# A two-layer decoder trunk on one core: where copies, low parts, value writes and filler steps stand inside the attention's passes over the heads

## The chip, the core and the metric

The kernel runs on one core of one Trainium2 chip. A core has five engines that work side by side, each on its own list of instructions in the order in which they were written down: TensorE (PE in the profile, with the weight loads as PEld), VectorE (DVE), ScalarE (ACT), GpSimd (POOL) and SyncE (SP, which here only issues DMA transfers). Between engines only semaphores order the work: an instruction whose operand isn't ready holds up everything behind it on its own engine, and nothing on the others. The metric is the device time of one execution in microseconds.

## The reference

A trunk of two layers over 1024 tokens of width 1024. Layer 0 mixes with a short gated convolution, layer 1 with dilated attention; each is followed by a SwiGLU network of width 2816, and a norm ends it. All is float32. The part that matters here is the attention of layer 1, with 16 heads of width 64:

```python
BRANCHES = ((128, 1), (512, 4), (2048, 16))     # window, dilation

def dilated_branch(q, k, v, rel_bias, window, dilation):
    ...
    s = jnp.einsum("brnqhd,brnkhd->brnhqk", qb, kk) * (HEAD_DIM ** -0.5)
    ...
    s = s + bias                                # T5 bucket of the distance
    s = jnp.where(mask, s, NEG_INF)
    lse = jax.nn.logsumexp(s, axis=-1)
    p = jnp.exp(s - lse[..., None])
    o = jnp.einsum("brnhqk,brnkhd->brnqhd", p, vv)
    ...
    return o, lse

def dilated_attention_mixer(h, w_qkv, w_out, rel_bias):
    q, k, v = ...                               # h @ w_qkv, 16 heads of 64
    for window, dilation in BRANCHES:
        o, l = dilated_branch(q, k, v, rel_bias, window, dilation)
        ...
    alpha = jax.nn.softmax(jnp.stack(lses), axis=0)
    o = jnp.sum(alpha[..., None] * jnp.stack(outs), axis=0)
    return o.reshape(bsz, seq, D_MODEL) @ w_out
```

The weights alpha of the three branches and the three softmaxes fall together: the result of a head is the sum of exp(s) v over the entries of all branches, divided by the sum of exp(s) over all of them. The kernel computes it so, with one maximum, one unnormalised sum `o` and one denominator `z` for each head.

## The kernel before

**Precision.** A product of the projections and of the SwiGLU networks is taken in three matmuls, high x high, high x low and low x high, of operands split in two. `split` (line 132) makes the two: ACT copies the source into `hi` (line 142), DVE subtracts it from the source into `lo` (line 143). `take` (line 171) hands the next weight of a fixed list `ops` to a product, and has the one after it loaded, and split, ahead (`ensure`, line 163).

**The attention, head by head.** `slot(n, ...)` (line 1727) is called for n = 0 to 16. Slot n writes down the scores of head n, the softmax of head n, and the values products of head n-1, mixed with steps of other matmuls that fill TensorE while the softmax is under way.

- `scores` (line 1547): seven banks of matmuls (line 1560 and others), each read by DVE, which adds the bias into `lf`, `lh`, `ld`, `lp`; then the maximum over all of them (`m`, line 1611) and GpSimd's maximum over the partitions (`mb`, line 1614).
- `softmax`: DVE subtracts `mb` (line 1622), ACT takes exp in place (line 1623), five times.
- `values` (line 1626): products of exp(s) with the values `vx`, whose columns hold 64 values and 64 ones, into two banks, one for each half of the tokens. Lines 1633 are its matmuls. The first twelve go over `lf` and `lh`; then `j` runs over eight blocks of 128 keys with `ld` and `lp`, four for each bank. At the end ACT copies `z` and `o` of both halves out of the two banks (lines 1656 and 1657).
- `finish` (line 1660): `z` of a pair of heads goes through DRAM (`zdram`), is turned into its reciprocal and comes back broadcast; `attended` multiplies it on `o` and writes the result to `odram`.

**Values.** `value_tiles(g, j)` makes the values of head group g (four heads), half j of the tokens: four blocks of eight times three matmuls, each copied out by ACT (`v`, line 1508). After the fourth it writes `v` to DRAM (`vdram`) with four DMAs on GpSimd's queue (line 1512). `load_values` (line 1515) reads them back in another order into `vx`, six DMAs on SyncE's queue (line 1520); for the slots up to 14 it is called from `load_kq` (line 1525), at the head of every second slot, between the loads of the keys and of the queries of the next head.

**The filler.** `dense` (function `fill`) is one long generator that gives a few matmuls with each `next`, a filler step: projections of queries and keys, values, and at the end `out_product` (line 1819), the first half of the output projection, which for each of eight output tiles loads up to three tiles of `x` from `spill` on SyncE (line 1825), multiplies, and adds the bank to `x` (`add_to_x`, line 492). `slot` takes 15 filler steps; what is left when the last slot is done runs behind it (`run(dense)`, line 1868).

**The order inside a slot.** For n up to LAG = 13 a slot is lagged: a first loop of eight passes takes one step of the scores and one filler step each; a second loop takes two steps of the values products, and at pass 3 the whole softmax, with the filler steps that are left spread over its passes. Slots 14 and 15 put the values products into the first loop, and slot 14 (`late` = 3) has no filler step in the first passes.

**Slot 12** (n = LAG-1, the block 13 of the change's title). Before it, `load_attended` loads the first four attended tiles `oin` from `odram`; the generator `halves` splits them into `first`, one with each `next(hook)`, in the second loop from pass SOFT = 4 on, that is behind the softmax:

```python
                if i >= SOFT:
                    next(hook, None)
                other(left * (i + 1) // 8 - left * i // 8)
...
        for n in range(H):
            if n == LAG - 1:
                done.update(load_attended(range(AO)))
            hook = halves() if n == LAG - 1 else iter(())
            slot(n, dense, 15, 3 if n == H - 2 else 0, hook)
            run(hook)
```

The output product's steps read these splits. With 15 steps a slot, its first step falls into slot 12.

**Queues.** SyncE carries the loads of weights (`raw`), keys, queries, values, bias tables, attended tiles and `x`; GpSimd the writes of `vdram`, `zdram`, `odram` and the reads of the reciprocals, between its maxima. A DMA that waits holds up those behind it on its queue.

Of the kernel before, what the change touches and what calls it, by code (L numbers as in the profile page):

```python
# [20 lines left out]
H = 16  # L21
# [72 lines left out]
def view(t, off, dims):  # L94
    return bass.AP(tensor=t.tensor, offset=t.offset + off, ap=[t.ap[0]] + [list(d) for d in dims])
# [3 lines left out]
def trunk(ctx: ExitStack, tc: tile.TileContext, x, gains_in, cwi, ck, cwo, wqkv, wo, relb,  # L99
# [29 lines left out]
    scratch = consts.tile([128, 1], F32)  # L129
    zcol = consts.tile([128, 2, 1], F32)  # L130

    def split(src, dst=None, eng=nc.vector):

        w = src.shape[1]
        if dst is None:
            if w <= HALF:
                t = page("w", F32R)
                dst = t[:, :w], t[:, HALF:HALF + w]
            else:
                dst = page("w_hi", F32R)[:, :w], page("w_lo", F32R)[:, :w]  # L140
        hi, lo = dst
        nc.scalar.activation(hi, src, AF.Copy)  # L142
        eng.tensor_tensor(out=lo, in0=src, in1=hi, op=ALU.subtract)  # L143
        return hi, lo


# [16 lines left out]
    def ensure(upto):  # L163
        while op_state[0] < min(upto + 1, len(ops)):
            key = ops[op_state[0] + 1][0] if op_state[0] + 1 < len(ops) else None
            if key in sums_of:
                sums_of.pop(key)()
            made[op_state[0]] = ops[op_state[0]][1]()
            op_state[0] += 1

    def take(key, ahead=1):
        i = op_state[1]
        assert ops[i][0] == key, (ops[i][0], key)
        ensure(i + ahead)
        op_state[1] += 1
        return made.pop(i)
# [198 lines left out]
    def run(*gens):  # L375
        for _ in zip(*gens):
            pass
        for g in gens:
            for _ in g:
                pass  # L380
# [1082 lines left out]
    def blk(j):  # L1463
        return (j // 4) * HALF + (j % 4) * 8

    def attention(norm, qk):
# [23 lines left out]
        def value_tiles(g, j):  # L1490

            if j == 0:
                wv[:] = [take(("v", g, i), 0) for i in range(2)]
            v = page("v")
            for b4 in range(4):
                if j and b4 in (1, 2):
                    ensure(op_state[1] + b4 - 1)
                t = 4 * j + b4
                b = bank()[:, :256]
                for k in range(KT):  # L1500
                    (hi, lo), (whi, wlo) = qk.h[j][k], wv[k // 4]
                    a, c = slice(b4 * 128, b4 * 128 + 128), slice(k % 4 * 256, k % 4 * 256 + 256)
                    nc.tensor.matmul(b, hi[:, a], whi[:, c], start=k == 0, stop=False)  # L1503
                    nc.tensor.matmul(b, hi[:, a], wlo[:, c], start=False, stop=False)  # L1504
                    nc.tensor.matmul(b, lo[:, a], whi[:, c], start=False, stop=k == KT - 1)  # L1505
                    if k % 2:
                        yield
                nc.scalar.activation(v[:, b4 * 256:b4 * 256 + 256], b, AF.Identity, scale=norm.r[:, t:t + 1])
                yield
            vd = vdram[g]  # L1510
            for r in range(4):
                nc.gpsimd.dma_start(bass.AP(vd.tensor, vd.offset + (512 * j + r) * 256,
                                          [[16 * 256, 32], [4 * 256, 4], [1, 256]]), v[32 * r:32 * r + 32])

        def load_values(p):
            src = vdram[p // 2]
# [109 lines left out]
        def values(p, a, st):  # L1626
            lf, lh, ld, lp = (st[n] for n in ("lf", "lh", "ld", "lp"))
            acc = [bank(), bank()]
            kd = [[128, 4], [1, 32]]
            b1 = [[32, 16], [1, 8]]  # L1630

            def mm(ih, off, dims, u, rhs, first=False, last=False):
                nc.tensor.matmul(view(acc[ih], off, dims), vx[:, u, 64 * a:64 * a + 128], rhs,  # L1633
                                 start=first, stop=last)

            for ih in range(2):
                for r4 in range(4):
                    mm(ih, r4 * 32, kd, 8 + r4, view(lf, ih * HALF + r4 * 32, kd), first=r4 == 0)
                    if r4 % 2:
                        yield  # L1640
            for r4 in range(4):
                mm(1, r4 * 32, kd, 12 + r4, view(lh, r4 * 32, kd))
                if r4 % 2:
                    yield
            for j in range(8):
                off = (j % 4) * 8
                mm(j // 4, off, b1, j, view(ld, blk(j), b1), last=False)
                if j:
                    mm(j // 4, off, b1, j - 1, view(lp, blk(j), b1), last=j % 4 == 3)
                yield  # L1650
            o, z = st["o"], st["z"]
            n0 = slice(64 * a, 64 * a + 64)
            z0 = slice(64 - 64 * a, 128 - 64 * a)
            for ih in range(2):
                s = slice(ih * HALF, (ih + 1) * HALF)
                nc.scalar.activation(z[n0, s], acc[ih][z0], AF.Copy)
                nc.scalar.activation(o[n0, s], acc[ih][n0], AF.Copy)
            yield

        def finish(p):  # L1660
# [66 lines left out]
        def slot(n, dense, ndense, late=0, hook=iter(())):  # L1727

            def other(k):
                for _ in range(k):  # L1730
                    next(dense, None)

            p, a = divmod(n, 2)
# [55 lines left out]
            for i in range(8):  # L1789
                next(pv, None)  # L1790
                next(pv, None)
                if i == (2 if n > LAG + 1 else 5):
                    attended()
                if lagged and a and ending and i == 6:
                    next(ending[-1])
                if not lagged and (i < FIN0 or i > SOFT):
                    next(extra, None)
                if i in (1, 2):
                    next(later, None)
                if i == (3 if lagged else SOFT):  # L1800
                    if n < H:
                        live[n] = new
                        run(softmax(new))
                if i >= SOFT:
                    next(hook, None)
                other(left * (i + 1) // 8 - left * i // 8)
            run(pv)
# [36 lines left out]
        def fill():  # L1844
            for kind, g in FILL[1:]:
                if kind == "qk":
                    yield from projections(g)
                else:
                    for j in range(2):
                        yield from value_tiles(g, j)  # L1850
            yield from out_product(0, range(AO), first)
# [4 lines left out]
                yield  # L1856

        dense = fill()
        for n in range(H):
            if n == LAG - 1:  # L1860
                done.update(load_attended(range(AO)))
            hook = halves() if n == LAG - 1 else iter(())
            slot(n, dense, 15, 3 if n == H - 2 else 0, hook)
            run(hook)
        acts.update(split_attended(load_attended(range(AO, 7))))
        ensure(ahead_ao)
        slot(H, dense, 15)
# [201 lines left out]
```

## Time and profile before

| | us |
|---|---|
| three runs | 2140.9, 2142.98, 2143.33 |
| median | 2142.98 |
| the profiled execution, its own time | 2143.59 |
| its span, first to last instruction | 2141.5 |
| mean granted clock of TensorE in it | 0.994 |

The span is what the views of the trace cut up; the time of the execution is 2.1 us longer. Times in the views count from the span's start. In the rows of a timeline the idle time of the engine just before an instruction stands in brackets with what released it; a row in which consecutive instructions of one form are gathered gives their number behind an x and their total length. "SPq" and "POOLq" rows are the issues of DMAs on SyncE's and GpSimd's queues. A tile's name is that of the program (`bank<-lf,vx` is a matmul of `lf` and `vx` into a bank).

### The profile page before, as it was taken

To read this page: it belongs to the slowest core of one execution; us is meant where nothing else is said; L and a number is where in the kernel's file an instruction comes from. 1 tells how busy PE (TensorE), PEld (TensorE's weight loads), DVE (VectorE), ACT (ScalarE), POOL (GpSimd) and SP (SyncE) were. 2 spreads that over 40 slices of the span, in tenths; PEclk is the share of its full clock that TensorE was granted. 3 is DMA by queue.
4 is the path that set the end of the run, shared out by engine and by line. 5 is a ranking of instruction groups with operands and counts; after the bars stand their busy time and mean duration, and the time that the engine had idled before them with its cause. 6 is when DMAs were issued, how large, how long until landed. Compare 5 with 4: busy or idle time off the path is not lost.

```text
span 2141.5 us, 31004 instructions
## 1 busy us (share of the span) xinstructions
PE 2108.1 (98%) x11086; PEld 1807.9 (84%) x11086; DVE 1744.0 (81%) x3272; ACT 1007.4 (47%) x1848; POOL 254.2 (12%) x370
## 2 busy tenths in 40 slices
PE   9999999999999999999999999899999999999998
PEld 7788878888888888877899989888788888888887
DVE  8798769988888888868967687777998888888876
ACT  7333426444444564335545544545543434356435
POOL 1000000110101000000323333221010101001000
PEclk9999999999999999999999999999999999999999
DMA  7322642233332576340767678755223333368432
GB/s 218 93 94 69 226 133 75 103 102 106 113 109 99 173 218 194 112 161 33 263 206 182 180 193 226 212 179 163 69 93 102 107 109 106 106 201 240 156 94 79
DMA packets 143354, 304.90 MB, mean 142 GB/s; under 512 B 48943, under 2 KB 55327, under 8 KB 143201
## 3 DMA queue, kind: packets, MB, share of 16 engines
q1 hardware_dynamic: 107488, 201.94, 31.3%
q0 software_dynamic: 28080, 86.29, 12.7%
q10 hardware_dynamic: 7632, 14.70, 1.8%
q8 instruction: 88, 1.44, 0.3%
q14 instruction: 66, 0.53, 0.1%
HBM read 212.48 MB, written 83.05 MB: 138 GB/s over the span
## 4 chain that ended last, share of the span: by engine, by line
PE 82%; DVE 7%; issue 3%; ACT 2%; DMA 2%; POOL 1%; SPq 0%; DVEq 0%; POOLq 0%; ACTq 0%
PE bank L563 19%; PE bank L561 19%; PE bank L562 19%; PE bank L371 4%; PE bank L372 4%; PE bank L370 4%; PE bank L653 3%; PE bank L656 3%; PE bank L655 3%; PE bank L1633 2%; POOL mb L1614 1%; PE bank L1503 1%; PE bank L1504 1%; PE bank L1505 1%; DVE w L143 1%
## 5 line engine op out<-in xcount | busy, mean ns | idle before, releaser
L563 PE MATMUL bank<-b,w 128*128 128x512 f32 x1952 | 761.7, 390 | 5.5 <-DVE w L143 5.3
L561 PE MATMUL bank<-b,w 128*128 128x512 f32 x1952 | 763.3, 391 | 2.1 <-ACT w L142 1.7
L562 PE MATMUL bank<-b,w 128*128 128x512 f32 x1952 | 761.1, 390 | 0.6 <-DVE b L872 0.6
L563 PEld LDWEIGHTS bank<-b,w 128*128 128x128 f32 x1952 | 366.8, 188 | 86.4 <-DVE w L143 10.2
L561 PEld LDWEIGHTS bank<-b,w 128*128 128x128 f32 x1952 | 367.0, 188 | 78.7 <-ACT w L142 2.8
L562 PEld LDWEIGHTS bank<-b,w 128*128 128x128 f32 x1952 | 366.9, 188 | 77.0 <-DVE b L872 1.8
L142 ACT ACTIVATE w<-combo 128x512 fp32r<-128x512 f32 (+2 forms) x488 | 249.2, 540 | 232.0 <-DVE combo L190 215.1
L143 DVE TENSOR_TENSOR w<-combo,w 128x512 fp32r<-128x512 f32 (+2 forms) x488 | 276.2, 579 | 39.4 <-ACT w L142 38.7
L567 ACT ACTIVATE part<-bank 128x512 f32<-128x512 f32 x186 | 110.7, 596 | 390.2 <-PE bank L563 388.5
L143 DVE TENSOR_TENSOR w<-raw,w 128x512 fp32r<-128x512 f32 (+2 forms) x342 | 189.5, 575 | 38.7 <-ACT w L142 38.7
L571 DVE TENSOR_TENSOR part<-part,bank 128x256 f32<-128x256 f32 (+1 forms) x366 | 170.5, 495 | 31.2 <-PE bank L563 16.7
L142 ACT ACTIVATE w<-raw 128x512 fp32r<-128x512 f32 (+2 forms) x342 | 166.7, 530 | 45.0 <-PE bank L563 12.2
L370 PE MATMUL bank<-w_hi,w 128*128 128x512 f32 (+1 forms) x400 | 153.8, 385 | 5.0 <-ACT w_hi L142 4.9
L371 PE MATMUL bank<-w_lo,w 128*128 128x512 f32 (+1 forms) x400 | 150.5, 376 | 1.2 <-DVE w_lo L143 1.2
L372 PE MATMUL bank<-w_hi,w 128*128 128x512 f32 (+1 forms) x400 | 150.1, 375 | 0.7 <-DVE w L143 0.7
L791 DVE TENSOR_TENSOR x<-x,bank 128x512 f32<-128x512 f32 x136 | 92.5, 680 | 29.1 <-PE bank L563 29.0
L492 DVE TENSOR_TENSOR x<-x,bank 128x512 f32<-128x512 f32 (+1 forms) x104 | 66.3, 642 | 59.6 <-PE bank L372 59.0
L190 DVE TENSOR_TENSOR combo<-raw 128x512 f32<-128x512 f32 (+1 forms) x172 | 111.1, 646 | 0.0
L370 PEld LDWEIGHTS bank<-w_hi,w 128*128 128x128 f32 x400 | 76.2, 191 | 18.8 <-ACT w_hi L142 5.4
L371 PEld LDWEIGHTS bank<-w_lo,w 128*128 128x128 f32 x400 | 76.0, 190 | 15.0 <-DVE w_lo L143 2.0
L372 PEld LDWEIGHTS bank<-w_hi,w 128*128 128x128 f32 x400 | 76.0, 190 | 14.5 <-DVE w L143 1.1
L554 DVE TENSOR_TENSOR b<-hin,b 128x512 fp32r<-128x512 f32 x126 | 79.4, 683 | 9.4 <-ACT b L553 9.4
(247 smaller groups left out, 3486.0 us busy)
## 6 DMA issues: line engine op xcount, KB each, us to landing
hin<-part SPq DMA_DIRECT2D x126, 256.0 KB
raw<-in_ffn_w_gate SPq DMA_DIRECT2D x44, 512.0 KB
raw<-in_ffn_w_up SPq DMA_DIRECT2D x44, 512.0 KB
part<-sum POOLq DMA_DIRECT2D x72, 256.0 KB, 2.3
raw<-in_ffn_w_down SPq DMA_DIRECT2D x48, 384.0 KB
raw<-in_attn_w_qkv SPq DMA_DIRECT2D x27, 512.0 KB
raw<-in_conv_w_in SPq DMA_DIRECT2D x24, 512.0 KB
part<-part POOLq DMA_DIRECT2D x36, 256.0 KB, 2.5
```

The costliest lines, as they stand in the source:

```text
L142: nc.scalar.activation(hi, src, AF.Copy)
L143: eng.tensor_tensor(out=lo, in0=src, in1=hi, op=ALU.subtract)
L190: eng.tensor_tensor(out=c, in0=a, in1=b, op=op)
L370: nc.tensor.matmul(b, whi[:, a], ahi[:, s], start=first, stop=False)
L371: nc.tensor.matmul(b, whi[:, a], alo[:, s], start=False, stop=False)
L372: nc.tensor.matmul(b, wlo[:, a], ahi[:, s], start=False, stop=last)
L561: nc.tensor.matmul(b, hi[:, a], bhi, start=start and k == 0, stop=False, skip_group_check=True)
L562: nc.tensor.matmul(b, hi[:, a], blo, start=False, stop=False, skip_group_check=True)
L563: nc.tensor.matmul(b, lo[:, a], bhi, start=False, stop=k == n - 1, skip_group_check=True)
L567: nc.scalar.activation(t, b, AF.Copy)
L571: nc.vector.tensor_tensor(out=t, in0=t, in1=b, op=ALU.add)
L791: nc.vector.tensor_tensor(out=X[n][:, half(h)], in0=X[n][:, half(h)], in1=b, op=ALU.add)
```

## The change

Five things, all inside the attention.

- `split` may put off the low part: while `put_lows` is a list, the subtraction is appended to it instead of written down, and `lows` writes them all down. It is called at the start of each filler step, and in `take`, behind the split of the weight that is handed out and ahead of the one after it. `put_lows` is a list for slots 0 to 15, and is emptied behind slots 12 and 15.
- `values` copies `z` and `o` of the first half as soon as its bank is complete (j = 3), four blocks ahead of the second half's.
- `value_tiles` writes down the four `vdram` DMAs directly behind the fourth `v`, where they stood one filler step later.
- `slot` calls the hook in the second loop's passes 0 to 3 where it did in 4 to 7.
- Slot 12 takes 12 filler steps where it took 15.

```diff
--- before.py
+++ after.py
@@ -129,6 +129,8 @@
     scratch = consts.tile([128, 1], F32)
     zcol = consts.tile([128, 2, 1], F32)
 
+    put_lows = None
+
     def split(src, dst=None, eng=nc.vector):
 
         w = src.shape[1]
@@ -140,7 +142,11 @@
                 dst = page("w_hi", F32R)[:, :w], page("w_lo", F32R)[:, :w]
         hi, lo = dst
         nc.scalar.activation(hi, src, AF.Copy)
-        eng.tensor_tensor(out=lo, in0=src, in1=hi, op=ALU.subtract)
+        low = lambda: eng.tensor_tensor(out=lo, in0=src, in1=hi, op=ALU.subtract)
+        if put_lows is None:
+            low()
+        else:
+            put_lows.append(low)
         return hi, lo
 
 
@@ -168,9 +174,15 @@
             made[op_state[0]] = ops[op_state[0]][1]()
             op_state[0] += 1
 
+    def lows():
+        while put_lows:
+            put_lows.pop(0)()
+
     def take(key, ahead=1):
         i = op_state[1]
         assert ops[i][0] == key, (ops[i][0], key)
+        ensure(i)
+        lows()
         ensure(i + ahead)
         op_state[1] += 1
         return made.pop(i)
@@ -1506,11 +1518,11 @@
                     if k % 2:
                         yield
                 nc.scalar.activation(v[:, b4 * 256:b4 * 256 + 256], b, AF.Identity, scale=norm.r[:, t:t + 1])
+                vd = vdram[g]
+                for r in range(4 * (b4 == 3)):
+                    nc.gpsimd.dma_start(bass.AP(vd.tensor, vd.offset + (512 * j + r) * 256,
+                                              [[16 * 256, 32], [4 * 256, 4], [1, 256]]), v[32 * r:32 * r + 32])
                 yield
-            vd = vdram[g]
-            for r in range(4):
-                nc.gpsimd.dma_start(bass.AP(vd.tensor, vd.offset + (512 * j + r) * 256,
-                                          [[16 * 256, 32], [4 * 256, 4], [1, 256]]), v[32 * r:32 * r + 32])
 
         def load_values(p):
             src = vdram[p // 2]
@@ -1642,19 +1654,19 @@
                 mm(1, r4 * 32, kd, 12 + r4, view(lh, r4 * 32, kd))
                 if r4 % 2:
                     yield
+            o, z = st["o"], st["z"]
+            n0 = slice(64 * a, 64 * a + 64)
+            z0 = slice(64 - 64 * a, 128 - 64 * a)
             for j in range(8):
                 off = (j % 4) * 8
                 mm(j // 4, off, b1, j, view(ld, blk(j), b1), last=False)
                 if j:
                     mm(j // 4, off, b1, j - 1, view(lp, blk(j), b1), last=j % 4 == 3)
+                if j % 4 == 3:
+                    s = half(j // 4)
+                    nc.scalar.activation(z[n0, s], acc[j // 4][z0], AF.Copy)
+                    nc.scalar.activation(o[n0, s], acc[j // 4][n0], AF.Copy)
                 yield
-            o, z = st["o"], st["z"]
-            n0 = slice(64 * a, 64 * a + 64)
-            z0 = slice(64 - 64 * a, 128 - 64 * a)
-            for ih in range(2):
-                s = slice(ih * HALF, (ih + 1) * HALF)
-                nc.scalar.activation(z[n0, s], acc[ih][z0], AF.Copy)
-                nc.scalar.activation(o[n0, s], acc[ih][n0], AF.Copy)
             yield
 
         def finish(p):
@@ -1728,6 +1740,7 @@
 
             def other(k):
                 for _ in range(k):
+                    lows()
                     next(dense, None)
 
             p, a = divmod(n, 2)
@@ -1801,7 +1814,7 @@
                     if n < H:
                         live[n] = new
                         run(softmax(new))
-                if i >= SOFT:
+                if i < 4:
                     next(hook, None)
                 other(left * (i + 1) // 8 - left * i // 8)
             run(pv)
@@ -1856,12 +1869,18 @@
                 yield
 
         dense = fill()
+        nonlocal put_lows
+        put_lows = []
         for n in range(H):
             if n == LAG - 1:
                 done.update(load_attended(range(AO)))
             hook = halves() if n == LAG - 1 else iter(())
-            slot(n, dense, 15, 3 if n == H - 2 else 0, hook)
+            slot(n, dense, 12 if n == LAG - 1 else 15, 3 if n == H - 2 else 0, hook)
             run(hook)
+            if n == LAG - 1:
+                lows()
+        lows()
+        put_lows = None
         acts.update(split_attended(load_attended(range(AO, 7))))
         ensure(ahead_ao)
         slot(H, dense, 15)
```

The matmuls, their operands and their sums stay the same; only the place of the instructions in each engine's list differs.

## The prediction

> **What bounds the kernel now.** I read the page first, then TensorE's timeline with the releaser of each idle stretch, then the clock by windows, and at last the queues that end those stretches.
>
> ```profile
> span 2141.5 us, 31004 instructions
> PE 2108.1 (98%) x11086; PEld 1807.9 (84%) x11086; DVE 1744.0 (81%) x3272; ACT 1007.4 (47%) x1848; POOL 254.2 (12%) x370
> ```
>
> TensorE is the bound: 33 us of the span are idle. The sum below is made against the profiled execution, 2143.59 us, which lies 0.6 above the median of 2142.98. The change leaves the order of every instruction outside the attention (1090 to 1445 us) as it was, so the question is which of TensorE's waits there go and which come. "Slot n" is the pass of `slot` for head n; the "block 13" of the change is slot 12. TensorE's rows (start, length, line, tiles, count, idle time before and its releaser):
>
> ```profile
> 1291.06 1.13 PE L1633 MATMUL bank<-lf,vx 128*128 128x128 f32 x8 [1.09 <-issue]
> 1308.62 0.38 PE L1560 MATMUL bank<-qa,ka 128*128 128x256 f32 x1 [1.60 <-ACT o L1657]
> 1348.98 1.95 PE L1633 MATMUL bank<-lf,vx 128*128 128x128 f32 x16
> 1361.34 0.80 PE L370 MATMUL bank<-w_hi,w 128*128 128x512 f32 x1 [4.92 <-ACT w_hi L142]
> 1377.89 1.95 PE L1633 MATMUL bank<-lf,vx 128*128 128x128 f32 x16
> 1389.26 1.06 PE L1633 MATMUL bank<-lf,vx 128*128 128x128 f32 x8
> 1417.37 0.39 PE L1560 MATMUL bank<-qa,ka 128*128 128x256 f32 x1 [2.51 <-DVE x L492]
> ...
> ```
>
> The largest wait is 4.92 us in slot 12: the first output-product filler needs the high part of an attended tile. The three L1633 rows at 1348.98, 1377.89 and 1389.26 open the values products of slots 12, 13 and 14; they are my marks. The clock by windows (bounds, length, busy time of PE, PEld, DVE, ACT, POOL, granted clock, DMA share, GB/s):
>
> ```profile
> 1305.00:1312.00 7.00, 5.40 (x45) 5.20 (x45) 6.49 (x16) 5.75 (x11) 1.75 (x4) 1.00 0.05 18
> 1356.00:1361.30 5.30, 0.42 (x4) 0.23 (x3) 3.39 (x5) 4.53 (x7) 0.00 (x0) 0.85 0.27 61
> 1361.30:1366.50 5.20, 4.70 (x14) 3.81 (x15) 4.63 (x4) 4.33 (x7) 2.51 (x5) 0.50 0.25 102
> 1417.40:1421.10 3.70, 3.70 (x18) 3.70 (x19) 3.67 (x9) 0.00 (x0) 1.24 (x3) 0.54 0.51 175
> ```
>
> A wait costs twice: after 4.9 us of idleness the next 5.2 us run at 0.50, worth 2.6 us, and after 2.5 us of it 3.7 us run at 0.54, worth 1.7. After 1.60 us the clock stays at 1.00.
>
> **The change part by part.** *Copies of z and o.* Where the exps stand directly ahead of them on ACT they cannot come sooner: the wait of 1.60 at 1308.62 stays. They pass a `v`, `kq_hi` or weight split in three slots, where no wait of TensorE hangs on them. No gain; the loss is in slot 11, below.
>
> *Low parts a step later.* One place gains.
>
> ```profile
> 1287.93 2.36 DVE L143 TENSOR_TENSOR w_lo<-raw,w_hi 128x1024 fp32r<-128x1024 f32 x2 [2.40 <-ACT w_hi L142]
> ```
>
> DVE sat behind ACT here with two bias additions of slot 9 queued behind, and TensorE's bank waited for them (the 1.09 above). They now go first. At most that wait and its follow-up, 1.6 us, is won; but 17 us on, at 1308.62, TensorE waits for ACT, whose chain through POOL moves by at most 0.6. I take -0.5 (0 to -1.6).
>
> *Values written behind their copy.* `vdram` writes of the third group, first half, now stand ahead of slot 11's all-reduce on POOL instead of behind it.
>
> ```profile
> 1333.11 0.58 POOL L1668 DMA_DIRECT2D zc<-zdram  x1 [5.58 <-DMA zdram<-z]
> 1333.72 3.18 POOL L1614 PARTITION_ALL_REDUCE mb<-m  x1
> 1336.78 2.19 POOL L1512 DMA_DIRECT2D vdram<-v  x4
> ...
> 1352.10 3.22 POOL L1614 PARTITION_ALL_REDUCE mb<-m  x1 [3.10 <-DVE m L1611]
> ...
> 1364.55 2.20 POOL L1512 DMA_DIRECT2D vdram<-v  x4
> ```
>
> Four issues take 2.2 us, and the all-reduce had no slack on POOL: it ends 2.2 later. DVE's subtractions of slot 11 follow it, then ACT's exps, then on ACT z, o, v, w where it was v, w.
>
> ```profile
> 1336.93 1.22 DVE L1622 TENSOR_TENSOR lf<-lf,mb 128x1024 f32<-128x1024 f32 x1 [4.58 <-POOL mb L1614]
> 1342.84 0.69 DVE L143 TENSOR_TENSOR w<-raw,w 128x512 fp32r<-128x512 f32 x1 [1.87 <-ACT w L142]
> 1351.23 0.69 DVE L1611 TENSOR_TENSOR m<-m,lp 128x512 f32<-128x512 f32 x1
> ...
> 1378.10 0.41 DVE L1597 TENSOR_TENSOR ld<-bank,bias 128x256 f32<-128x256 f32 x1
> 1379.35 0.69 DVE L1611 TENSOR_TENSOR m<-m,lp 128x512 f32<-128x512 f32 x1
> 1383.46 1.22 DVE L1622 TENSOR_TENSOR lf<-lf,mb 128x1024 f32<-128x1024 f32 x1 [2.20 <-POOL mb L1614]
> ```
>
> ```profile
> 1342.19 0.62 ACT L142 ACTIVATE w<-raw 128x512 fp32r<-128x512 f32 x1
> 1342.83 0.59 ACT L1656 ACTIVATE z<-bank 64x512 f32<-64x512 f32 x1
> ...
> 1360.24 1.04 ACT L142 ACTIVATE w_hi<-oin 128x1024 fp32r<-128x1024 f32 x1
> 1361.19 0.45 ACT L1508 ACTIVATE v<-bank,r 128x256 f32<-128x256 f32 x1
> ...
> 1384.72 1.06 ACT L1623 ACTIVATE lf<-lf 128x1024 f32<-128x1024 f32 x1 [14.30 <-DVE lf L1622]
> ```
>
> DVE's low part at 1342.84 already waited for ACT's w. With 2.2 and two copies of 0.6 more it comes 3.4 later, and slot 12's additions and maxima, packed behind it up to the m at 1351.23, come 3.3 later. So slot 12's all-reduce starts at 1355.4 instead of 1352.10.
>
> *Splits ahead of the softmax, 12 steps.* The first three high parts now run on ACT before the exps and no output product stands in slot 12: the 4.92 and its 2.6 of slow clock go. But the last `v`, whose write feeds slot 13's values, moves back on ACT: ahead of it now stand the fourth split (1.0) and four copies (2.4), where it had one split. From the end of the exps at 1360.24 + 3.3 = 1363.5 it ends at 1367.3, and the four writes start there at the earliest, against 1364.55: 3.2 later. SyncE's rows (issues, and its wait from the table of waits), then two transfers of the chain of waits and a line of the page's DMA issues:
>
> ```profile
> 1348.82 2.50 SPq L1825 DMA_DIRECT2D x<-spill  x3
> ...
> 1370.83 0.38 SPq L1520 DMA_DIRECT2D vx<-vdram  x1
> ...
> 1377.46 0.56 SPq L1453 DMA_DIRECT2D bias<-tables  x1
> ...
> SPq L1520 <- DMA vdram<-v: 16.6, 1, 16.6
> ```
>
> ```profile
> 1288.87 4.59 DMA bias<-tables
> ...
> 1410.00 6.49 DMA zc<-zdram
> ```
>
> ```profile
> part<-sum POOLq DMA_DIRECT2D x72, 256.0 KB, 2.3
> ```
>
> The values' loads wait for those writes, so they issue at 1370.83 + 3.2 = 1374.0, and taking 4.1 to land, as the writes did (1366.75 to 1370.83), slot 13's values products open at about 1377.7 (bounds 2.3 and 6.5: 1376.3 to 1380.5). TensorE is there much sooner: the 28.9 us between the first two marks, less 4.9 idle, 2.8 for the slow window (4.70 busy at half speed in 5.20) and 2.1 of fillers, plus some 4 of short waits for slot 12's delayed copies and low parts, give 1372. A new wait of about 6 us, and the mark comes at the same time as before, with three filler steps less done.
>
> *The x reads.* The first output-product step also issues the three `x<-spill` loads. In slot 12 they were out at 1348.82, with nothing behind them that hurt. In slot 13 they stand on SyncE behind two ka, six vx (which wait), three q and two bias loads: from the first vx to the last bias is 1370.83 to 1378.02, so x goes out at 1374.0 + 7.2 = 1381.2. Landing takes between 2.3 and 6.5; a 512 KB load just behind the bias pair is nearest to the 4.59, and I take 5: 1386.3. DVE's addition of the first product to x waits for that, and behind it on DVE stand the last four bias additions and two maxima of slot 13, 1.94 us (1378.10 to 1380.04): the all-reduce starts at 1389.6 at best. From the old start (3.24 before the lf at 1383.46) to the end of the lf exp at 1385.78 are 5.56 us; so slot 14's values products, which read lf, open at about 1395.3 instead of 1389.26. TensorE gets there at some 1377.7 + 10.9 = 1388.6, and as slot 14 has no filler in its first steps, it waits 6 us.
>
> ```profile
> 1381.43 0.23 PE bank L370
> ```
>
> *Three steps moved.* A step is three matmuls of 0.23, so 3 x 0.7 = 2.1 us are still to be done after the mark of slot 14; they end up behind the last slot.
>
> **The sum:** +6.0 at the mark of slot 14, +2.1 for the steps, +2.0 for the slow clock behind slot 14's wait (1.7 to 2.6 by the two windows above; before had none there), -0.5 in slot 9, and -0.5 in slot 15, where the wait of 2.51 comes one bank later and I make it 2.0 with the slow stretch kept (-2.2 if the clock holds, 0 if not shorter). 2143.6 + 9.1 = 2152.7, which is 2152 beside the median. With 2.3 and 6.5 for x the mark moves by -2.7 and +1.5, with no shift from slot 11 by -3.3.
>
> [...]
>
> **The rivals.** *The x reads land in time* (a). Then DVE does not stand, slot 13's softmax is ready, only the values' wait stays, and slot 14's mark comes at 1390.6: +1.3 + 2.1 + 0 - 0.5 - 0.5, so 2145. For it: x can be quick (2.3). Against: SyncE takes them in order behind loads that wait for the values' write.
>
> *Neither new wait* (b), faster. If the values' write landed before 1365, the slot 12 wait with its slow clock (4.9 + 2.8) and slot 9's 1.6 would be won whole: 2134. It decides where `vdram` lands more than 7 us sooner than my 1374. For it: ACT has idle time ahead of slot 12's exps. Against: the last v stands behind them.
>
> *No shift from slot 11* (c): the all-reduce loses nothing, the x reads still come late: 2152 - 3.3 = 2149, slower all the same.
>
> **How the numbers follow.** My forecast 0.58, (c) 0.18, (a) 0.14, (b) 0.10. About 0.2% (4.3 us) is what a measurement of this kernel tells from no change: (b) is faster, 0.10; (a) and a little of (c) lie within, 0.16; the rest is slower, 0.74. The forecast's own range is 2149 to 2156; to leave out no more than 2 in 10 it goes down to (a), and up by the slow landing and a second slow window: 2144.5 to 2157.
>
> **What would show it.** Right: no wait before the first L370 product in slot 12; about 6 us before slot 13's values products, released by `vx<-vdram`; about 6 before slot 14's, released by ACT's lf exp, with DVE's x addition idle for `x<-spill` before it; half clock after both. The all-reduce of slot 11 behind the four writes. Wrong: slot 14's products opening within 2 us of the last fillers, or slot 13's all-reduce starting before 1385.

## The result and the profile after

| | us |
|---|---|
| changed kernel, six runs | 2145.89 to 2150.37, median 2147.98 |
| kernel before, six runs | 2137.71 to 2143.33, median 2141.15 |
| ratio | 1.0037, 95% interval 1.0027 to 1.0047 |
| changed kernel, the profiled execution | 2145.89, span 2144.0 |

The change costs 6.8 us between the medians. The forecast was 9.1 and 2152. TensorE's timeline of the changed kernel (start, length, line, tiles, count, idle time before and its releaser; its lines lie 2 to 13 further down than before):

```profile
1354.98 0.39 PE L382 MATMUL bank<-w_hi,w 128*128 128x512 f32 x1
...
1360.85 0.50 PE L383 MATMUL bank<-w_lo,w 128*128 128x512 f32 x1 [2.71 <-DVE w_lo L145]
...
1373.84 3.76 PE L1645 MATMUL bank<-lf,vx 128*128 128x128 f32 x16 [5.09 <-DMA vx<-vdram]
...
1392.50 2.08 PE L1645 MATMUL bank<-lf,vx 128*128 128x128 f32 x8 [4.79 <-ACT lf L1635]
...
1414.09 1.05 PE L1645 MATMUL bank<-lf,vx 128*128 128x128 f32 x8
```

The first output product (1354.98) waits no longer; the wait of 4.92 is gone. Three came: 2.71 at a low part, 5.09 at slot 13's values products and 4.79 at slot 14's. Slot 15's 2.51 is gone too. Behind each of the three, the windows (bounds, length, busy time of PE, PEld, DVE, ACT, POOL, granted clock, DMA share, GB/s) show the slow clock:

```profile
1360.80:1364.80 4.00, 3.85 (x14) 3.06 (x15) 3.21 (x5) 3.90 (x7) 0.55 (x1) 0.60 0.02 6
1373.80:1378.20 4.40, 4.36 (x18) 4.25 (x19) 0.00 (x0) 0.00 (x0) 0.00 (x0) 0.50 1.09 267
1392.50:1396.20 3.70, 3.70 (x19) 3.70 (x20) 3.70 (x9) 3.49 (x6) 0.56 (x1) 0.57 1.07 240
```

The way to the 5.09 goes over ACT, POOL and SyncE, each by its own timeline:

```profile
1359.59 1.03 ACT L1635 ACTIVATE lp<-lp 128x384 f32<-128x384 f32 x2
1360.52 1.04 ACT L144 ACTIVATE w_hi<-oin 128x1024 fp32r<-128x1024 f32 x1
1361.58 0.59 ACT L1667 ACTIVATE z<-bank 64x512 f32<-64x512 f32 x1
...
1364.02 0.47 ACT L1520 ACTIVATE v<-bank,r 128x256 f32<-128x256 f32 x1
```

```profile
1351.55 4.04 POOL L1626 PARTITION_ALL_REDUCE mb<-m  x1 [6.79 <-DVE m L1623]
...
1364.82 2.20 POOL L1523 DMA_DIRECT2D vdram<-v  x4
...
1386.88 3.22 POOL L1626 PARTITION_ALL_REDUCE mb<-m  x1 [15.84 <-DVE m L1623]
```

```profile
1370.15 0.38 SPq L1532 DMA_DIRECT2D vx<-vdram  x1
...
1376.76 0.56 SPq L1465 DMA_DIRECT2D bias<-tables  x1
1377.43 1.68 SPq L1838 DMA_DIRECT2D x<-spill  x3
```

Behind the exps stand the fourth split and four copies, then v; POOL writes from 1364.82, SyncE reads from 1370.15, and the x reads go out behind the last bias load. DVE's timeline shows what stands behind x:

```profile
1351.29 1.22 DVE L145 TENSOR_TENSOR w_lo<-oin,w_hi 128x1024 fp32r<-128x1024 f32 x1
1352.42 2.91 DVE L145 TENSOR_TENSOR w_lo<-oin,w_hi 128x1024 fp32r<-128x1024 f32 x1
...
1358.51 1.15 DVE L1634 TENSOR_TENSOR lp<-lp,mb 128x384 f32<-128x384 f32 x2
1359.58 1.22 DVE L145 TENSOR_TENSOR w_lo<-oin,w_hi 128x1024 fp32r<-128x1024 f32 x1
...
1383.49 0.69 DVE L504 TENSOR_TENSOR x<-x,bank 128x512 f32<-128x512 f32 x1 [14.38 <-DMA x<-spill]
...
1386.01 0.69 DVE L1623 TENSOR_TENSOR m<-m,lp 128x512 f32<-128x512 f32 x1
...
1387.21 2.10 DVE L145 TENSOR_TENSOR w<-raw,w 128x512 fp32r<-128x512 f32 x1
```

For 14.38 us DVE does nothing, with four bias additions and two maxima of slot 13 behind it; the all-reduce starts at 1386.88, and exps and slot 14 follow. The third split's low part (1359.58), which TensorE needed at 1358.14, stands behind the softmax's subtractions; that is the wait of 2.71.

One profile of each kernel is not enough to read 6.8 us. The table gives the starts of the first values product of each slot, counted from the attention's first score matmul, for two executions of either kernel (the second ones are from the experiments below). That first matmul itself lay between 1111.4 and 1115.9 in the profiles of this study, before anything that the change touches; so spans are not compared here, but these distances are.

| us from the first score matmul | before | before, second | changed | changed, second |
|---|---|---|---|---|
| slot 10 | 196.78 | 199.95 | 195.17 | 194.76 |
| slot 12 | 233.45 | 236.62 | 232.94 | 232.50 |
| slot 13 | 262.36 | 264.29 | 260.44 | 259.66 |
| slot 14 | 273.73 | 275.65 | 279.10 | 278.95 |
| slot 15 | 293.71 | 295.64 | 300.69 | 301.83 |
| slot 16 | 318.36 | 316.83 | 320.92 | 322.06 |
| first matmul of the SwiGLU network | 380.02 | 378.60 | 384.62 | 385.76 |
| last matmul | 1020.02 | 1018.13 | 1024.66 | 1025.28 |

By the last row the change costs 4.6 in the first pair and 7.2 in the second.

### The profile page after: what moved, and what is told of

Its sections match the earlier page's. It is cut to its first block, busy times and chain, and to the rows that moved or that the text cites. A ratio compares the mean times of both kernels' runs of the same rounds, so it can differ in the third digit from the quotient of the medians.

```text
span 2144.0 us, 31018 instructions
## 1 busy us (share of the span) xinstructions
PE 2109.2 (98%) x11086; PEld 1810.4 (84%) x11086; DVE 1749.0 (82%) x3272; ACT 1007.9 (47%) x1848; POOL 254.4 (12%) x370
## 4 chain that ended last, share of the span: by engine, by line
PE 85%; DVE 7%; DMA 3%; issue 2%; ACT 2%; POOL 1%; SPq 0%; DVEq 0%; ACTq 0%; POOLq 0%
PE bank L575 19%; PE bank L573 19%; PE bank L574 19%; PE bank L382 4%; PE bank L384 4%; PE bank L383 4%; PE bank L665 3%; PE bank L668 3%; PE bank L667 3%; PE bank L1645 2%; PE bank L1515 1%; PE bank L1516 1%; PE bank L1517 1%; POOL mb L1626 1%; DVE w L145 1%
```

## The experiments

All ratios are to the kernel before, run on the same chip, with 95% intervals. The edits are to the changed kernel unless it says "before".

**The x reads alone, early.**

```diff
             if n == LAG - 1:
                 lows()
+                for k in range(3):
+                    X[k] = page("x")
+                    nc.sync.dma_start(X[k], spill[k])
```

> The changed kernel, with the three x<-spill loads of the first output-product tiles issued at the end of slot 12 instead of behind slot 13's values and query loads; nothing else moves. My theory (two waits in a row: the values' write late for slot 13, the x reads late for slot 14): the wait of 5.09 us before slot 13's values products stays within 1 us, the 14.4 us in which DVE's x addition waits for x<-spill goes, slot 14's wait of 4.79 falls below 1, and the mark of slot 14 comes 4 to 6 us sooner. Slot 15's old wait for zc (2.5 and its slow clock, 4.2 together) may then come back, so the time is 2 to 6 us below the changed kernel: 1.0005 to 1.0025 of before. Rival one (slot 14's wait has nothing to do with x, it is only handed on from slot 13): slot 14's wait stays above 4 and the time is that of the changed kernel, 1.0037. Rival two (the early copies and late low parts are the loss): the same, 1.0037.

Measured: 0.9999 (0.9990 to 1.0008). TensorE's and DVE's timelines:

```profile
1361.65 0.50 PE L383 MATMUL bank<-w_lo,w 128*128 128x512 f32 x1 [1.84 <-DVE w_lo L145]
...
1374.10 3.75 PE L1645 MATMUL bank<-lf,vx 128*128 128x128 f32 x16 [4.68 <-DMA vx<-vdram]
...
1387.96 0.50 PE L1645 MATMUL bank<-lf,vx 128*128 128x128 f32 x3
```

```profile
1369.84 0.68 DVE L504 TENSOR_TENSOR x<-x,bank 128x512 f32<-128x512 f32 x1
```

The addition of x waits for nothing, slot 14's products open without a wait, slot 13's keep theirs. The wait of slot 14 is the x reads'; both rivals fall. The gain was larger than I wrote (8 us on the changed kernel by the ratios, not 2 to 6), as slot 15's wait did not come back.

**The values alone, early.** All four filler steps of slot 12's second loop ahead of its softmax, so that the last v is copied before the exps.

```diff
+                if n == LAG - 1 and i == 2:
+                    other(left)
                 if i == (3 if lagged else SOFT):
...
-                other(left * (i + 1) // 8 - left * i // 8)
+                if n != LAG - 1:
+                    other(left * (i + 1) // 8 - left * i // 8)
```

> The changed kernel, with the four filler steps that slot 12's second loop takes all ahead of its softmax, so that the last v is copied and written before ACT's exps and not behind them and five more ACT instructions. My theory: the vdram write starts near 1356 instead of 1364.8, the loads of vx 6 to 8 us sooner, and the wait before slot 13's values products goes. The x loads, still behind these on SyncE, come 6 to 8 us sooner too, but TensorE is there 5 us sooner: 3 to 5 us of wait stay before slot 14's products. The mark of slot 14 comes about 8 sooner, slot 15's old wait comes back with up to 4.2: 4 us below the changed kernel (2 to 8), 1.000 to 1.003 of before. Rival one (only the values' wait, slot 14's is its echo): both waits go, 8 us or more below the changed kernel. Rival two (the copies and low parts): 1.0037.

Measured: 0.9994 (0.9985 to 1.0003). The same two timelines:

```profile
1362.60 0.80 PE L383 MATMUL bank<-w_lo,w 128*128 128x512 f32 x1 [3.81 <-DVE w_lo L145]
...
1386.69 2.08 PE L1645 MATMUL bank<-lf,vx 128*128 128x128 f32 x8 [3.88 <-ACT lf L1635]
```

```profile
1377.68 0.69 DVE L504 TENSOR_TENSOR x<-x,bank 128x512 f32<-128x512 f32 x1 [8.82 <-DMA x<-spill]
```

The wait before slot 13's products is gone; the one before slot 14's stays at 3.88, with DVE waiting 8.82 for x. So the two waits stand behind one another on SyncE: each goes by itself, and x is late even when the values are not. The low part's wait grew to 3.81, which I had not written. The time came out below my range (1.000 to 1.003), as slot 15's wait did not come back here either.

**Fifteen steps, the rest of the change kept.**

```diff
-            slot(n, dense, 12 if n == LAG - 1 else 15, 3 if n == H - 2 else 0, hook)
+            slot(n, dense, 15, 3 if n == H - 2 else 0, hook)
```

> The changed kernel with 15 filler steps in slot 12 instead of 12, everything else of the change kept. My theory: the x loads go out near 1349 as before, the first three output products find their splits made ahead of the exps, so slot 12's wait of 4.92 does not come back; v stands behind the exps, one split and two copies on ACT, so that 1 to 4 us of wait stay before slot 13's values products; none before slot 14's. Slot 15's wait is there. The three steps are not left over. 3 us below before (1 to 6), 0.997 to 0.9995. Rival two (the loss is in the early copies and late low parts, or in the value writes ahead of slot 11's all-reduce, not in the steps): it stays slower than before, 1.001 to 1.004.

Measured: 0.9987 (0.9978 to 0.9995), faster than before. The three steps are back: from slot 16's mark to the SwiGLU network it takes 61.65 us, as before (61.66), against 63.70 in the changed kernel. The 1 to 4 us that I had left before slot 13's values products did not come, nor did slot 15's wait. A wait that I had not written did:

```profile
1362.08 0.79 PE L382 MATMUL bank<-w_hi,w 128*128 128x512 f32 x1 [4.63 <-ACT w_hi L144]
```

The fourth output product, in slot 13's first filler step, needs the one split that still stands behind the exps. The wait of 4.92 was not removed here, only moved one split on.

**Fifteen steps and early values.** The two edits above together, with the last three steps in passes 5 to 7.

```diff
+                if n == LAG - 1 and i == 2:
+                    other(12 - used)
                 if i == (3 if lagged else SOFT):
...
-                other(left * (i + 1) // 8 - left * i // 8)
+                if n != LAG - 1:
+                    other(left * (i + 1) // 8 - left * i // 8)
+                elif i > 4:
+                    other(1)
```

> The changed kernel with 15 filler steps in slot 12, four of them ahead of the softmax (so v is copied before the exps) and three, the first output products, in the second loop's last passes. My theory: no wait before slot 12's output products, none before slot 13's values products, none before slot 14's; slot 15's of about 2.5 stays. The mark of slot 14 comes 6 us sooner than before, counted from the attention's start: 0.9965 to 0.9985 of before, 2 to 4 us below the run with 15 steps alone. Rival two (the copies, low parts or writes cost it): not below before.

Measured: 0.9993 (0.9984 to 1.0002), short of what I expected and not shown to be below before. TensorE's and DVE's timelines:

```profile
1367.14 0.79 PE L383 MATMUL bank<-w_lo,w 128*128 128x512 f32 x1 [5.65 <-DVE w_lo L145]
```

```profile
1364.73 1.22 DVE L1733 TENSOR_TENSOR o<-o,z 128x1024 f32<-128x1024 f32 x1
1365.87 2.35 DVE L145 TENSOR_TENSOR w_lo<-oin,w_hi 128x1024 fp32r<-128x1024 f32 x2
```

No filler step comes between the third split and the softmax any more, so its low part, put off to the next step, lands behind all subtractions on DVE. Values and x are in time: no wait opens the products of slots 13 and 14. The wait of 5.65 is the largest left between slots 11 and 14, and I put the lost gain down to it; rival two was right about the low parts. The profiled execution is the slowest of its eleven, 3.3 above their median.

**The kernel before, profiled again.** No edit.

> The kernel before, unchanged, profiled a second time. Question: whether slot 15's wait of 2.51 us and its slow clock (with them 24.65 us between the values marks of slots 15 and 16; 20.23 in the changed kernel and in the runs with early x, 15 steps, early values) belong to the kernel or to one execution. Theory A (order: the 8 KB read zc<-zdram goes out 1.7 us behind a 512 KB x<-spill read and takes 6.49 us, and that order follows from the kernel): the wait is there again, the distance of the marks is 23 to 25. Theory B (a race that falls either way from one execution to the next): the distance is 20 to 21.5. The attention's start lies anywhere between 1111 and 1116. Ratio 1.000.

Measured: 1.0000 (0.9991 to 1.0009), a profiled execution with a span of 2136.5. Slot 15 to slot 16 takes 21.19 us, not 24.65, so theory B. Of the DMA views, from 1403 to 1417 of the first execution (6.5, in the first of the two fences) and from 1402 to 1413 of the second:

```profile
zc<-zdram POOLq DMA_DIRECT2D x1, 8.0 KB, 6.5
```

```profile
zc<-zdram POOLq DMA_DIRECT2D x1, 8.0 KB, 3.9
```

In the first the read goes out at 1410.00, 1.7 us behind a 512 KB read of x, and in the second at 1407.94; why it was quicker there is not shown. The second execution waits longer at slot 10, and the 5.35 us behind that wait run at a clock of 0.50:

```profile
1305.85 0.58 PE L1560 MATMUL bank<-qa,ka 128*128 128x256 f32 x1 [4.13 <-ACT o L1657]
```

**The writes alone.** The kernel before, with the four `vdram` writes behind the fourth v as in the diff of the change.

> The kernel before with one part of the change: the four vdram writes written down directly behind the fourth v. My theory: slot 11's all-reduce stands behind four issues of 2.2 us and is 2 us late, the exps of slots 11 and 12 are 2 to 3 late, and slot 12's wait for the first attended tile's high part grows from 4.92 to 6.5 to 8: 2 to 4 us slower than before, 1.0008 to 1.002. Rival (c) (the all-reduce loses nothing that TensorE sees): within 1 us of before.

Measured: 1.0004 (0.9995 to 1.0012).

```profile
1360.20 0.79 PE L370 MATMUL bank<-w_hi,w 128*128 128x512 f32 x1 [6.19 <-ACT w_hi L142]
```

Slot 12's wait grew, to 6.19 from 4.92 and from 3.72 in the two executions of before, but the time moved by no more than is measured. Here rival (c) is nearer than I was, though the interval reaches into my range, which began at 1.0008.

**The softmax late in slot 12, 15 steps.** All that ACT has to do in slot 12 then stands ahead of the exps.

```diff
-                if i == (3 if lagged else SOFT):
+                if i == (7 if n == LAG - 1 else 3 if lagged else SOFT):
...
-            slot(n, dense, 12 if n == LAG - 1 else 15, 3 if n == H - 2 else 0, hook)
+            slot(n, dense, 15, 3 if n == H - 2 else 0, hook)
```

> The changed kernel with 15 steps in slot 12 and slot 12's softmax written down in the last pass of the second loop (i = 7) instead of i = 3: all four splits, the copies of z and o, and v then stand ahead of the exps on ACT, in time in which ACT waits for the all-reduce, and the low parts ahead of the subtractions on DVE. My theory: the wait of 4.63 us that the run with 15 steps still has in slot 13's first filler (the fourth split behind the exps), with 1.5 to 2.6 of slow clock behind it, goes or falls below 2; the values of slot 13 are loaded 5 us sooner, so no new wait before them, or one of at most 2. 3 to 6 us below the run with 15 steps: 0.9955 to 0.9975 of before. Rival (DVE, which does low parts ahead of the subtractions, hands the delay on to slot 13's or 14's products): a new wait of 3 or more there, no gain on the run with 15 steps, 0.998 to 0.9995.

Measured: 0.9949 (0.9936 to 0.9963), a little faster than I expected. ACT's and DVE's timelines:

```profile
1347.73 1.99 ACT L144 ACTIVATE w_hi<-oin 128x1024 fp32r<-128x1024 f32 x2
...
1352.13 0.47 ACT L1520 ACTIVATE v<-bank,r 128x256 f32<-128x256 f32 x1
...
1354.02 0.59 ACT L1668 ACTIVATE o<-bank 64x512 f32<-64x512 f32 x1
1357.92 1.06 ACT L1635 ACTIVATE lf<-lf 128x1024 f32<-128x1024 f32 x1 [3.31 <-DVE lf L1634]
```

```profile
1349.30 6.32 DVE L145 TENSOR_TENSOR w_lo<-oin,w_hi 128x1024 fp32r<-128x1024 f32 x4
```

Four splits, four copies and v are done in time in which ACT waited for the all-reduce anyway; ACT then waits another 3.31 us before the exps start. No wait over 1 us is left between slots 11 and 14.

**The softmax late in all lagged slots.** Slot 12 takes 15 steps here too.

```diff
-                if i == (3 if lagged else SOFT):
+                if i == (7 if lagged else SOFT):
```

> The same, with the softmax in the last pass of the second loop in all lagged slots (0 to 13). Theory: the copies of z and o then come ahead of the exps, so that TensorE's waits for ACT's o at the head of slots 3, 7 and 10 (1.2, 1.2 and 1.6 to 2.9 us, the last with a slow clock) go as well: another 2 to 5 us, 0.993 to 0.997 of before. Rival (the weights' high parts, v and kca then stand between, and the exps end too late for the next slot's values products): new waits for ACT's lf or ld before values products in several slots, 1.00 or slower.

Measured: 2123.46 us, 0.9924 (0.9912 to 0.9937), again a little faster than I expected. The window from the attention's start to about slot 16's mark, of this kernel and of the second executions of the kernel before and of the changed one (bounds, length, PE busy first, granted clock third from the end):

```profile
1110.00:1413.00 303.00, 300.78 (x2261) 285.43 (x2259) 234.23 (x425) 153.97 (x221) 99.91 (x102) 1.00 0.76 206
```

```profile
1110.00:1429.00 319.00, 306.41 (x2257) 289.20 (x2256) 233.20 (x425) 154.01 (x221) 98.57 (x102) 0.98 0.73 196
```

```profile
1110.00:1434.00 324.00, 306.15 (x2247) 289.33 (x2246) 235.79 (x423) 153.94 (x220) 99.46 (x102) 0.97 0.71 193
```

The attention takes 303 us instead of 319, TensorE idles for 2.2 of them, and the granted clock is 1.00, against 0.98 and 0.97.

**The changed kernel, profiled again.** No edit.

> The changed kernel, unchanged, a second profile. Theory: the waits that follow from the order are there again: 4 to 6 us before slot 13's values products for vx<-vdram, 4 to 6 before slot 14's for ACT's lf, the distance of the values marks of slots 13 and 14 above 17 (11.4 in the kernel before). Slot 10's wait for ACT's o may be anything from 1.5 to 4.1, as it was in other executions. Ratio 1.0025 to 1.0045. If the two waits are a matter of one execution, the distance is below 14.

Measured: 1.0037 (1.0024 to 1.0049); waits of 2.73, 4.92 and 5.43 at the three places, and 19.29 us between the marks of slots 13 and 14. They follow from the order.

**Hook, 12 steps and writes, without the early copies and late low parts.** These three go together: with 12 steps, writes at their old place would stand behind the loads that read them, so the step count was not tried alone.

```diff
-                if i >= SOFT:
+                if i < 4:
                     next(hook, None)
...
-            slot(n, dense, 15, 3 if n == H - 2 else 0, hook)
+            slot(n, dense, 12 if n == LAG - 1 else 15, 3 if n == H - 2 else 0, hook)
```

(to the kernel before, with the writes as above)

> The kernel before with three parts of the change (hook in passes 0 to 3, 12 steps in slot 12, vdram writes behind the fourth v), without the early copies of z and o and without late low parts. My theory: the whole loss is here: the wait before slot 13's values products is 5 to 8 us (TensorE comes sooner, as slot 12's wait for the third low part goes), slot 14's mark lies as in the changed kernel within 1.5 us: 1.0025 to 1.0045 of before. Rival two (copies and low parts cost part of it): 1.0015 or less.

Measured: 1.0046 (1.0032 to 1.0060); my range ended at 1.0045.

```profile
1374.79 2.02 PE L1633 MATMUL bank<-lf,vx 128*128 128x128 f32 x16 [3.09 <-DMA vx<-vdram]
...
1394.37 2.08 PE L1633 MATMUL bank<-lf,vx 128*128 128x128 f32 x8 [7.50 <-ACT lf L1623]
```

The whole loss is here, as expected; the shares of the two waits are not (3.09 and 7.50, where I had 5 to 8 for the first). The fourth split's wait (2.41) and a slow stretch in slot 13, a clock of 0.54 over 7.39 us from 1362.81, bring TensorE later to the values. Slot 14's mark lies 3.8 us behind the changed kernel's (282.86 from the attention's start, against 279.10) and not within 1.5; 3.5 of that is there at slot 10's mark (198.67 against 195.17).

**Early copies and late low parts alone.** The kernel before, with these two parts of the diff.

> The other two parts alone: early copies of z and o, and low parts a filler step later, in the kernel before. My theory: up to 0.6 us each at slots 3 and 9, taken back by slot 10's wait for ACT's o in part; slots 12 to 14 as before: 0.9985 to 1.0003 of before. Rival two: 1.001 or more.

Measured: 1.0013 (1.0004 to 1.0022), slightly slower; my expectation was wrong and rival two right. ACT's timeline:

```profile
1358.03 1.02 ACT L1635 ACTIVATE lp<-lp 128x384 f32<-128x384 f32 x2
1359.06 0.59 ACT L1667 ACTIVATE z<-bank 64x512 f32<-64x512 f32 x1
1359.66 0.59 ACT L1668 ACTIVATE o<-bank 64x512 f32<-64x512 f32 x1
1360.28 1.06 ACT L144 ACTIVATE w_hi<-oin 128x1024 fp32r<-128x1024 f32 x1
```

With the splits still behind the softmax, the early z and o slip in between the exps and the first split, 1.2 us, and TensorE's wait for it is 6.13. The half clock behind that wait lasts longer as well: at least 8.0 us at 0.50 (1361.39 to 1369.39), where it was 5.2 in the first execution of the kernel before. How much of that comes from the copies and how much from the low parts was not tried, and the profiled execution, 2145.23, lies 4.2 above its run's median. In the changed kernel that split stands ahead of the exps, and the 1.2 us are not paid.

**The late softmax alone.** The kernel before with the softmax in pass 7 of the lagged slots and the hook in passes 0 to 3.

> The kernel before with the softmax in pass 7 of the second loop in the lagged slots, and the hook in passes 0 to 3; 15 steps, copies, low parts and writes as before. If the place of the softmax is what counts, this is 0.992 to 0.9945 of before, within 3 us of the run that had the change's other parts as well. If the early copies and the late low parts are needed for it, it is 0.996 or more.

Measured: 2124.76 us, 0.9934 (0.9921 to 0.9946). Two edited lines in the kernel before give nearly all of it; the change's other parts are not needed.

## Why the prediction was right, and where it was off

**The two waits.** Right, with their causes. I had 6 before slot 13's values products and 6 before slot 14's; 5.09 and 4.79 came, 4.92 and 5.43 in the second execution. The run with early x and the run with early values took them away one at a time. Slot 14's mark moved by 5.4 from the attention's start (279.10 against 273.73) in the profile that my sum was made against; the forecast was 6.0 less 0.5 from slot 9. That it comes so near is partly luck. Slot 10's mark had come 1.6 sooner, not 0.5, and from slot 13's mark to slot 14's it took 18.66 and 19.29, where I had 17.4 (11.37 and 6.0): x took 6.1 us to land (1377.43 to 1383.49), where I took 5, and in the second execution DVE stood 14.62 us for it. Between the second executions slot 14's mark moved by only 3.3, mostly because the kernel before had its long wait at slot 10 there.

**The three steps.** I wrote 2.1; 63.70 less 61.66 is 2.0, and 15 steps take it away.

**Slips in the working.** Three of its figures don't follow from the ones beside them: the values' writes come 2.75 later by 1367.3 less 1364.55, not 3.2; 1374.0 and 4.1 make 1378.1, not 1377.7; and 1378.10 to 1380.04 holds only two of the four additions, which with the two maxima took 2.6 us in the changed kernel (1384.10 to 1386.70), not 1.94. The first two slips cancel, and 1389.6 already fits 2.6 rather than 1.94, so the sum does not move by more than half a us.

**The slow clock in slot 14.** I wrote 2.0. The clock was 0.57 over 3.7 us in the first execution and 0.50 over five us in the second (1390.97 to 1395.97). From slot 14's mark to slot 15's it took 21.59 and 22.88, against 19.98 and 19.99: 1.6 and 2.9.

**Slot 15.** The term that was mis-sized: I had -0.5, "with the slow stretch kept", and the step from slot 15 to 16 fell from 24.65 to 20.23, by 4.4. That is 3.9 of the 4.5 by which the sum missed in that profile. Most of this was not the change's to remove: of two executions of the kernel before, one has the wait and one doesn't (24.65 and 21.19), and the 8 KB read took 6.5 us in the one and 3.9 in the other. I took a wait of one execution for one of the kernel. The last 1.0, from 21.19 to 20.23, is in both executions of the changed kernel; in the first of them the 8 KB read goes out ahead of the last read of x (1414.43 and 1415.10) and DVE has it 2.0 us later. That this order gives the 1.0 was not tried by itself. The execution with the wait of 2.51, 2143.59, also lies 2.4 above the median of six runs, 2141.15.

**Slot 11.** I wrote that the writes delay its all-reduce by 2.2, and with it slot 12's by 3.3. Slot 12's starts 238.15 us after the attention's start (1351.55 in the row above), against 236.57: 1.6 later. Counted from slot 10's mark it is 42.98 against 39.79, 3.2 later (4.4 between the second executions), so the shift was there; TensorE's marks came 1.6 sooner at slot 10, which hides half of it.

**Slot 12.** "Some 4 of short waits": one wait of 2.71, and 4.0 us at a clock of 0.60, 1.6 lost. The size is right. I had named late copies and low parts, but not the place: the third low part, written down behind the subtractions because the next filler step comes behind the softmax.

**Copies and low parts.** "No gain" for the copies held only with the splits ahead of the exps; alone with the low parts they cost 0.13%. What that run won at slot 9's mark (172.64 from the attention's start, against 175.53 and 174.01) is not to be seen at slot 10's (197.57, against 196.78 and 199.95). I had written that it would be taken back there, but slot 10's wait is anything from 1.60 to 4.13 in the kernel before, so these runs can't size it.

**The rivals.** (a) fell: DVE stood 14.38 us for the x reads. (b), neither new wait, needed the values' write 7 us sooner; the late softmax in slot 12, with 15 steps, made it (writes at 1353.47 instead of 1364.82) and gave 11.1 less than the kernel before, where I had written 9.3 less (2134). (c) fell by slot 11's shift, though the writes alone cost no more than is measured.

## What to carry to other kernels

On an engine that takes its list in order, place the long op that waits for others (here the exps behind an all-reduce) behind the short ones that are ready: two edited lines that do this gave 0.7% where five moved parts lost 0.4%. A filler step carries more than its matmuls; when it moves, its loads go to another place in their queue and its additions to another place on DVE, and both can stall work that has nothing to do with it, here the maxima of slot 13, which stood behind 14.38 us of idle DVE. Profile the kernel before twice: a wait that one execution shows may not be there in the next, as the 2.51 us at slot 15 were not.

## What the runs showed of the hardware

**The clock does not follow the length of a wait alone.** Windows behind TensorE's waits of 1.84 (early x, slot 12) and of 3.09 (hook and 12 steps, slot 13; both rows above):

```profile
1361.65:1365.20 3.55, 3.55 (x12) 2.79 (x13) 2.81 (x4) 3.45 (x7) 0.15 (x1) 0.57 0.02 5
```

```profile
1374.80:1379.80 5.00, 5.00 (x37) 4.73 (x38) 0.00 (x0) 0.00 (x0) 0.00 (x0) 1.00 1.09 246
```

Behind the shorter wait the clock was 0.57, behind the longer 1.00. The fifteen waits of 3.72 to 7.50 us inside the attention that these timelines show were each followed by a first us at 0.50. From 1.84 to 3.09 it went either way. The windows behind 2.04 (early values and 15 steps, slot 10), 2.41 (hook and 12 steps, slot 13), 2.51 and 2.71 (the kernel before and the changed one, above) ran at 0.62, 0.54, 0.54 and 0.60; those behind 2.05 (the writes alone, slot 10) and 2.99 (hook and 12 steps, slot 10) at 1.00. Single waits of 1.09, 1.15 and 1.60 in the kernel before and of 1.47 and 1.78 in the changed one were followed by 1.00. Two waits of 1.24 and 0.48, with four matmuls between, were followed by a us at 0.59 and two at 0.50 once (hook and 12 steps, slot 3); the same pair in the kernel before, 1.23 and 0.49, by 1.00. What decides it is not shown.

**Low parts beside the all-reduce: the one that started first took no longer than alone, the other did.** The low part at 1351.29 started 0.26 us ahead of the all-reduce at 1351.55: it took 1.22 us, as the one at 1359.58 does with no all-reduce beside it, and the all-reduce took 4.04, where the one at 1352.10 in the kernel before, with DVE idle, took 3.22. The low part at 1352.42 came behind both and took 2.91. The low part at 1387.21 started 0.33 behind the all-reduce at 1386.88: now the all-reduce took 3.22, and the low part 2.10 where its like took 0.69 (1342.84 in the kernel before). It was done at 1389.31, 0.8 us before the all-reduce was. Why the second one took longer is not shown.

**The same read took 3.9 and 6.5 us** in two executions of one kernel, and 3.5 us of TensorE's time went with it (24.65 against 21.19 from slot 15 to 16).
